# Matrix product with leaky ReLU: the last turn of the first region as two products of quarters, and three measures and sums moved

## The chip, the core and the metric

The kernel runs on one NeuronCore of a Trainium2 chip. The metric is device time in microseconds (us) of one execution. The engines are named as in the profile: PE (TensorE, the matrix multiplier), PEld (its weight loads), DVE (VectorE), ACT (ScalarE), POOL (GpSimd) and SP (SyncE). In this kernel POOL and SP mainly issue DMA transfers; POOL's casting loads bring float32 in as float16.

## The reference

```python
a, b: 4096 x 4096 float32, drawn from a normal distribution; alpha = 0.01
x = np.matmul(a, b)
return np.where(x > 0, x, alpha * x)
```

## The kernel before, in words

**Regions.** The output is cut into 16 regions of 1024 rows by 1024 columns, named (g, j): g is the group of rows, j the pair of column blocks of 512. All of one group is done before the next. The depth of 4096 is cut in two halves of two units of 1024 (KC = 8 slices of 128 each), so that a region's A is 2 x 2 blocks (A11 to A22, each 512 rows by 2048) and its B too (b11 to b22, each 2048 by 512; the first index is the half of the depth, the second the 512 columns).

**Seven products.** All regions but the first are computed by a Strassen-Winograd scheme with seven block products instead of eight. `PRODUCTS` (L684) gives their order: a11 with b11, a12 with b21, s2 with t2, s3 with t3, s1 with t1, a22 with t4, s4 with b22. The s are sums of blocks of A (`sum_a`, L598), the t are sums of blocks of B (`b_sum`, L618); DVE makes both, and t3, t2, t4 and t1 overwrite b12, b11, b21 and t2 in place. A block product is 64 matmuls of 128x512 (L864). From the second group on, many block products are again split into seven products of quarters (`quarter_product`, L781): 16 matmuls of 128x256 each, with further sums of quarters (`sums_of_a`, `sums_of_b`).

**The first region** (0, 0) is computed plainly, as loads come in: `TURNS` lists four turns over the units of the depth, for the upper and the lower 512 rows in turn. Each turn fills all eight PSUM banks; `spill` (L322) then adds a bank to `part[h]`, the float32 tile of the rows of half h, in SBUF. The loop over `steps` (L464) runs over the turns' units; the last turn is its steps 6 and 7, the lower rows with units 2 and 3, that is A22 with b21 and b22: 128 matmuls (L290). During step 5 DVE transposes A22 piece by piece (L143) as its loads land. `leave_first` (L333) puts the result through leaky ReLU; the upper rows are stored by SP at once, the lower ones by POOL at the start of region (0, 1).

**Measures.** The seven-product scheme is used only if the data is even enough: `Measure` (L222) squares a block on ACT (four squares of 128x2048), adds the squares on DVE (L246, L249, L250), folds them (`fold`, L253) and keeps greatest, least and sum in `stats`. A `judge` at the end decides whether a plain product in a second branch is to run instead. `EARLY` and `MEASURED` (L676 and on) say in which region which block is measured. Before, A21 (`first_measure`), b21 and b22 of pair 0 (`last_columns`) are measured in the first region and at the start of (0, 1).

**Order.** Each engine runs its instructions in the order in which the program writes them (`manual_schedule`), and so does each DMA queue; semaphores hold an instruction until what it needs is there. Tiles come from pools with few buffers: `x` (3), `c` (2 for each of two tags), `a16` (3), `b` (2 for each tag). A tile's buffer is written again only when its last reader is done, a DMA that stores it included. So the order of DVE's work ahead of a product, and the stores that it waits for, decide when the product can start.

**Region (0, 1)** (i = 0 in the loop at L819). DVE makes s1, s2, t3 and t2, a measure's sums, s3, the leaky ReLU of the first product, then s4, t4 and t1 (two `b_sum` each). `keep_half` (L833) stores b21 and b22 to DRAM for later groups through SP; t4 overwrites b21. s1 and s2 live in the `x` pool, where the first region's `room` and `part` tiles were.

**Region (1, 0)**, the second of its group: `sums_of_s3` (L760), then `sums_of_a(g, "s1", ...)` (L725, its sums in L736): four sums of quarters of s1 into tiles of the `a16` pool, each stored to DRAM (`kept_qs`); then t3 and t2 for each half of the depth. Region (3, 0) makes the same four sums, but loads its t2 and t3.

**The end.** `seventh_at_the_end` (L1130) computes the last block product by quarters and spreads the adds and leaky ReLUs over it; its last quarter product goes row block by row block (`by_row`).

## Time and profile before

| what | value |
|---|---|
| time, three runs | 1522.14 us median (1522.13 to 1524.24) |
| profiled execution | 1522.71 us, span 1520.9 us |
| mean granted clock | 0.998 |
| first region up to its last turn | 0 to 93.1 us |
| its last turn | 93.1 to 120.7 us |
| region (0, 1) | 120.7 to 221.5 us |
| region (1, 0) | 508.4 to 599.9 us |
| region (3, 0) | 1245.9 to 1335 us |
| last matmul ends | 1513.7 us |

Rows of the timeline give the start in us, the duration in us, the engine, the line of the program, the operation, output <- input with partitions x elements, and the count of merged instructions; in brackets stands how long the engine had been idle before and what ended that. A merged row's duration runs from the first start to the last end. Matmuls are pipelined: a matmul's duration is longer than the distance between two starts, and the distance is what counts. Rows of waits read: who waited <- for whom: us in total, times, longest. Rows that begin with a stretch A:B give its length and the busy time and count of PE, PEld, DVE, ACT and POOL, then the granted PE clock (1.00 is full), the mean busy share of the DMA engines and GB/s. "DMA to landing" gives smallest, median and greatest time from issue to landing of the transfers of one place.

### The profile page before, as it was taken

Reading aid. Unit: us, or ns where it says so; the run is one execution under the profiler, and the core shown is the slowest. Engines: PE = TensorE matmul, PEld = TensorE weight load, DVE = VectorE, ACT = ScalarE, POOL = GpSimd, SP = SyncE. Lnnn points to the kernel's source line nnn. Section 1 sums busy time; section 2 is a strip of 40 time slices with the busy share of each in tenths; the row PEclk is TensorE's granted clock in tenths of the full one; section 3 lists DMA queues with packets and bytes.
Section 4 is the critical chain, followed back from the end, with each engine's and each line's share of the span. In section 5 each row is a group of like instructions: output and inputs, shape, how many; then the busy total and the mean of one; then the engine's idle time right before and its main releaser. Section 6 shows DMA issues by size and latency. Waiting matters only on the chain.

```text
span 1520.9 us, 24417 instructions
## 1 busy us (share of the span) xinstructions
PE 1507.9 (99%) x9883; PEld 965.9 (64%) x9883; DVE 1201.1 (79%) x1250; ACT 524.4 (34%) x905; POOL 252.3 (17%) x418
## 2 busy tenths in 40 slices
PE   9999999999999999999999999999999999999998
PEld 4444444444445667585544688888454488888887
DVE  4589866786697597798779698987887786998797
ACT  2441434647511123225571122323574111242321
POOL 5632110134201102012320101000331000100000
PEclk9999999999999999999999999999999999999999
DMA  9999797899889999999898989979989697987845
GB/s 245 187 217 209 203 277 212 132 215 191 201 346 237 297 290 295 286 293 291 202 259 328 267 319 248 351 241 322 242 215 304 247 279 275 258 293 188 348 146 171
DMA packets 193965, 384.97 MB, mean 253 GB/s; under 512 B 17585, under 2 KB 126385, under 8 KB 178738
## 3 DMA queue, kind: packets, MB, share of 16 engines
q0 software_dynamic: 115584, 108.03, 44.9%
q1 hardware_dynamic: 71058, 245.53, 43.1%
q10 hardware_dynamic: 7200, 29.76, 5.0%
q8 instruction: 79, 1.29, 0.3%
q14 instruction: 44, 0.36, 0.1%
HBM read 359.66 MB, written 129.50 MB: 322 GB/s over the span
## 4 chain that ended last, share of the span: by engine, by line
PE 63%; DVE 1%; DMA 0%; issue 0%; DVEq 0%
PE ps L787 31%; PE ps L864 23%; PE ps L845 9%; DMA s<-kept_s 0%; DVE c L320 0%; DVE b L1354 0%; DVE b L620 0%; DVE c L1144 0%; DVEq L620 0%; DVEq L1144 0%; DVEq L320 0%
## 5 line engine op out<-in xcount | busy, mean ns | idle before, releaser
L864 PE MATMUL ps<-b,a 128*128 128x512 f16 x1984 | 431.6, 379 | 0.0
L864 PEld LDWEIGHTS <-a 128*128 128x128 f16 x1984 | 194.1, 98 | 233.2
L864 PE MATMUL ps<-b,s 128*128 128x512 f16 x1472 | 323.2, 380 | 2.2 <-DVE b L620 2.2
L864 PEld LDWEIGHTS <-s 128*128 128x128 f16 x1472 | 144.4, 98 | 177.0 <-DVE b L620 2.7
L564 POOL DMA_DIRECT2D b<-in_b_dram x120 | 88.9, 746 | 864.2 <-PE ps L864 312.5
L787 PEld LDWEIGHTS <-q 128*128 128x128 f16 x2192 | 214.0, 98 | 26.0 <-issue 0.7
L620 DVE TENSOR_TENSOR b<-b 128x4096 f16<-128x4096 f16 x82 | 185.9, 2286 | 45.0 <-DMA b<-in_b_dram 33.2
L887 ACT COPY c<-ps 128x512 f32<-128x512 f32 x164 | 86.1, 595 | 288.6 <-PE ps L864 187.7
L143 DVE STREAM_TRANSPOSE a<-a 128x512 uint32<-128x512 uint32 (+2 forms) x120 | 126.9, 1105 | 66.7 <-DMA a<-in_a_dram 66.7
L134 POOL DMA_DIRECT2D a<-in_a_dram x252 | 137.4, 552 | 246.6 <-ACT junk L639 82.9
L787 PEld LDWEIGHTS <-a 128*128 128x128 f16 x1440 | 140.9, 98 | 17.4
L320 DVE SCALAR_TENSOR_TENSOR c<-c 128x1024 f32<-128x1024 f32 (+2 forms) x123 | 142.0, 1193 | 10.0 <-ACT c L887 9.7
L639 ACT ACTIVATE junk<-a 128x512 bf16<-128x512 f16 x192 | 121.2, 631 | 70.3 <-DMA a<-in_a_dram 65.1
L787 PE MATMUL ps<-b,q 128*128 128x256 f16 x1088 | 128.1, 273 | 0.0
L237 ACT ACTIVATE sq<-b 128x2048 bf16<-128x2048 f16 x56 | 104.1, 1910 | 63.1 <-DVE sq L246 56.1
L787 PE MATMUL ps<-q,q 128*128 128x256 f16 x1024 | 119.0, 273 | 0.1
L290 PE MATMUL ps<-b,a 128*128 128x512 f16 x512 | 112.2, 379 | 0.5 <-ACT a L387 0.2
L787 PE MATMUL ps<-b,a 128*128 128x256 f16 x912 | 107.4, 273 | 0.0
L787 PEld LDWEIGHTS <-s 128*128 128x128 f16 x960 | 93.9, 98 | 12.3 <-issue 0.9
L290 PEld LDWEIGHTS <-a 128*128 128x128 f16 x512 | 49.7, 98 | 60.8 <-issue 1.4
L845 PE MATMUL ps<-b,a 128*128 128x256 f16 x640 | 70.7, 273 | 0.0
L845 PE MATMUL ps<-b,s 128*128 128x256 f16 x640 | 70.7, 273 | 0.0
(147 smaller groups left out, 1363.7 us busy)
## 6 DMA issues: line engine op xcount, KB each, us to landing
b<-in_b_dram POOLq DMA_DIRECT2D x128, 512.0 KB, 13.6
out_dram<-c SPq DMA_DIRECT2D x118, 512.0 KB, 8.2
a<-in_a_dram POOLq DMA_DIRECT2D x244, 128.0 KB, 5.8
b<-kept_half SPq DMA_DIRECT2D x28, 1024.0 KB, 12.4
b<-kept SPq DMA_DIRECT2D x20, 1024.0 KB, 9.3
q<-kept_qs ACTq DMA_DIRECT2D x40, 512.0 KB, 7.7
s<-kept_s SPq DMA_DIRECT2D x18, 1024.0 KB, 7.2
q<-kept_qs SPq DMA_DIRECT2D x28, 512.0 KB, 6.6
```

Of the source, the lines that this page charges most:

```text
L134: nc.gpsimd.dma_start(a16[32 * q:32 * q + 32], src.rearrange("(g i) w -> i g w", i=32))
L143: nc.vector.transpose(part.rearrange("p c m e -> p c (m e)").bitcast(U32) .rearrange("p c (g i) -> p g c i", i=32), src[:, :, i * n:(i + 1 ...
L237: nc.scalar.activation(to, self.parts[n], SQUARE)
L290: nc.tensor.matmul(ps, a_cols(at[0, h, u], c, mt, (h, u) == (0, 0)), bt[0, u, nt][:, c, :], start=first, stop=last,)
L320: nc.vector.scalar_tensor_tensor(t, t, alpha, t, op0=MULT, op1=MAX if alpha <= 1 else MIN)
L564: nc.gpsimd.dma_start(t[:, c:c + 4, :], b_rows(j, u, c, 4, nt, g > 0))
L620: nc.vector.tensor_tensor(f(to), f(x0), f(x1), op)
L639: nc.scalar.activation(junk, piece[:, q, :], SQUARE, accum_out=to[:, 4 * n + q:4 * n + q + 1])
L787: nc.tensor.matmul(to[m], xq[:, c // 2, rows, c % 2], yq[:, c, :], start=first and c == 0 and m < banks, stop=c == KC - 1, skip_group_chec ...
L845: nc.tensor.matmul(to, a_cols(operand(g, name, k), c, q // 2 * 2 + m), B(half, nt, k)[:, c, q % 2 * HALF:(q % 2 + 1) * HALF], start=False, ...
L864: nc.tensor.matmul(banks[mt], a_cols(t, c, mt, t is first_a), B(half, nt, k)[:, c, :], start=first and (k, c) == todo[0], stop=(k, c) == t ...
L887: nc.scalar.copy(to, bank)
```

## The change

Four things are changed.

1. The last turn of the first region leaves the plain loop. `leave_in_quarters` computes A22 with b21 and A22 with b22 as seven products of quarters each: 14 products of 16 matmuls of 128x256 (224) in place of 128 of 128x512. DVE makes four sums of A22's quarters (`sums`, in tiles of the `c` pool) and three new quarters of b22; those of b21 are made after step 4, in `room`. ACT copies PSUM banks so that a partial result can go on in two places, and `more` adds banks to `part[1]` in SBUF. The leaky ReLU and the stores of `part[0]` come after this turn instead of within it.
2. A21 is measured in (0, 1) instead of in the first region; b21 of pair 0 in (1, 0), ahead of the four sums of s1; b22 of pair 0 in (3, 0), in tiles of the `c` pool, between the third and the fourth of these sums.
3. In (0, 1) the stores of b21 (`keep_half((0,))`) are issued ahead of s3, and s4 is made after t1 instead of before t4.
4. At the end, the last quarter product writes its two row blocks to two banks (one new, `apart`, into which ACT copies what was there) instead of one.

```diff
@@ leave_first
-        if h == 0:
-            nc.sync.dma_start(out[row:row + P, :2 * NT], kept)
-        else:
-            stores.append((out[row:row + P, :2 * NT], kept))
+        nc.sync.dma_start(out[row:row + P, :2 * NT], kept)
@@ the loop over the first region's steps
+    t_of_b21 = {n: room[:, n - 1] for n in range(1, 5)}
...
-    for i in range(1, len(steps)):
+    for i in range(1, len(steps) - last_turn):
...
-            if i == 5 and g > 1:
+            if i == 5 and 1 < g < MT:
                 spill(t, h, leaves, banks)
...
         if i == 4:
             for m in first_columns:
                 m.end()
+            q = quarters_of_first(0)
+            f = lambda n: t_of_b21[n].rearrange("p (c n) -> p c n", n=HALF)
+            nc.vector.tensor_tensor(f(3), q[1, 1], q[0, 1], SUB)
+            nc.vector.tensor_tensor(f(2), f(3), q[0, 0], ADD)
+            nc.vector.tensor_tensor(f(1), q[1, 1], f(2), SUB)
+            nc.vector.tensor_tensor(f(4), q[1, 0], f(2), SUB)
-        if i == 5:
-            first_measure = Measure(0, halves(at[0, 1, 0]) + halves(at[0, 1, 1]), True, room)
-            first_measure.begin()
-            last_columns = [
...
-    last_columns[0].end()
@@ regions in which blocks are measured
     EARLY = {
-        (1, 3): [B11], (1, 1): [B11], (2, 3): [B21], (2, 1): [B12], (3, 1): [B21],
+        (1, 0): [B21], (1, 3): [B11], (1, 1): [B11], (2, 3): [B21], (2, 1): [B12], (3, 1): [B21],
     }
+    IN_C = (3, 0)
@@ sums_of_a
         make(3, (0, 0), (1, 0), SUB)
+        if ahead_of_4:
+            ahead_of_4()
         make(4, (0, 1), 2, SUB)
@@ new
+    def leave_in_quarters():
...
+        for nt in range(2):
+            quarter_product(x[0, 0], b[nt][0, 0], into(chain[nt]), True)
+            nc.scalar.copy(one[nt], chain[nt])
+        for nt in range(2):
+            quarter_product(x[0, 1], b[nt][1, 0], into(one[nt]))
+        tt(fx(1), xf[1, 0], xf[1, 1], ADD)
+        tt(fx(2), fx(1), xf[0, 0], SUB)
+        more(0, 0, 0, one[0])
+        tt(fx(3), xf[0, 0], xf[1, 0], SUB)
+        tt(b[1][0, 1], b[1][1, 1], b[1][0, 1], SUB)
+        tt(fx(4), xf[0, 1], fx(2), SUB)
...
+        new_t(2, turned[1](3), b[1][0, 0], ADD)
+        spill(2, 0, MT - 1, banks)
+        new_t(1, b[1][1, 1], turned[1](2), SUB)
+        for nt in range(2):
+            t = turned[nt]
+            shared, other = new_bank(4 + 2 * nt), new_bank(5 + 2 * nt)
+            if nt == 0:
+                quarter_product(sx(1), t(1), into(shared), True)
+            quarter_product(sx(2), t(2), into(chain[nt]))
+            nc.scalar.copy(other, chain[nt])
+            if nt:
+                quarter_product(sx(1), t(1), into(shared), True)
+            for r in range(2):
+                more(nt, r, 1, shared)
+            quarter_product(sx(3), t(3), into(chain[nt]))
+            if nt:
+                new_t(4, b[1][1, 0], turned[1](2), SUB)
+            more(nt, 1, 1, chain[nt])
+            nc.scalar.copy(one[nt], chain[nt])
+            quarter_product(sx(4), b[nt][1, 1], into(other))
+            more(nt, 0, 1, other)
+            quarter_product(x[1, 1], t(4), into(one[nt]))
+            more(nt, 1, 0, one[nt])
+            if nt == 0:
+                more(1, 0, 0, one[1])
+        for nt in range(2):
+            for r in range(2):
+                leaky(part[1][:, 2 * r:2 * r + 2, nt * NT:(nt + 1) * NT])
+            if nt == 0:
+                for mt in range(MT):
+                    leave_first(0, mt)
...
@@ seventh_at_the_end
+            ends = [of_y(2, 0), part(apart, 0)]
+            nc.scalar.copy(ends[1], of_y(3, 0))
...
-            quarter_product(x[1, 1], t(4), onto(y, 1, 0), by_row=True)
+            quarter_product(x[1, 1], t(4), ends, by_row=True)
@@ the loop over regions
+            c_places = [c_pool.tile([P, 2048], BF16, name="sq", tag=f"c{n % 2}") for n in range(4)]
+            first_measure = Measure(0, halves(at[0, 1, 0]) + halves(at[0, 1, 1]), True, c_places)
+            for n in range(4):
+                first_measure.square(n)
...
+        in_c = (g, j) == IN_C
+        if in_c:
+            m = measure(i, *B22)
+            m.room = [c_pool.tile([P, 2048], BF16, name="sq", tag=f"c{n}") for n in (side, side, 1 - side, 1 - side)]
+            for n in range(4):
+                m.square(n)
+        if second_of_group:
+            sums_of_a(g, "s1", new_a16, m.end if in_c else None)
...
-            last_columns[1].end()
+            first_measure.end()
...
-        if g == 1 and j in OTHERS:
+        if g == 1 and j in OTHERS or (g, j) == (0, LAST):
             keep_half((0,))
...
         if (g, j) == (0, LAST):
-            keep_half()
-        if i == 0:
-            sum_a(g, "s4")
+            keep_half((1,))
...
             for k in ks:
                 b_sum(B(0, 0, k), B(1, 1, k), B(0, 0, k), SUB)
+        if i == 0:
+            sum_a(g, "s4")
```

More of the change, by code (lines that the diff above doesn't have):

```diff
@@ L815, in next_a, with block, more, new_t @@
         return made
+    def leave_in_quarters():
+        x = quarters_of_a(0, "a22")
+        xf = {key: by_chunk(q) for key, q in x.items()}
+        sums = {n: c_pool.tile([P, QUARTER], DT, name="sums", tag=f"c{n % 2}") for n in range(1, 5)}
+        sx = lambda n: a_quarter(sums[n])
+        fx = lambda n: by_chunk(sums[n])
+        b = [quarters_of_first(nt) for nt in range(2)]
+        t3_there = {3: b[1][0, 1]}
+        t_of_b22 = {}
+        turned = [lambda n: b_quarter(t_of_b21[n]), lambda n: t3_there[n] if n in t3_there else b_quarter(t_of_b22[n])]
+        tt = nc.vector.tensor_tensor
+        chain = [new_bank(0), new_bank(2)]
+        one = [new_bank(1), new_bank(3)]
+        def block(nt, r, n):
+            cols = slice(nt * NT + n * HALF, nt * NT + (n + 1) * HALF)
+            return part[1][:, 2 * r:2 * r + 2, cols]
+        def more(nt, r, n, bank):
+            nc.vector.tensor_add(block(nt, r, n), pair(bank), block(nt, r, n))
+        for nt in range(2):
[9 more added lines that the diff above has]
+        tt(fx(4), xf[0, 1], fx(2), SUB)
+        def new_t(n, x0, x1, op):
+            t_of_b22[n] = new_a16()
+            tt(b_quarter(t_of_b22[n]), x0, x1, op)
+        new_t(2, turned[1](3), b[1][0, 0], ADD)
[29 more added lines that the diff above has]
+                    leave_first(0, mt)
+        for mt in range(MT):
+            row = (MT + mt) * P
+            stores.append((out[row:row + P, :2 * NT], part[1][:, mt, :]))
@@ L1128, in first_in_quarters, with seventh_at_the_end @@
                 nc.scalar.copy(z[to], bank)
-        def seventh_at_the_end(y, one, other, tq, sq, one_more):
+        def seventh_at_the_end(y, one, other, tq, sq, one_more, apart):
             pairs, kept = new_c(side)
```

35 lines of the change are left out of this document (13 added, 22 removed).

## The prediction, before the result was known

> **What bounds the kernel now.** I read the table of engines first, then what TensorE (PE) waited for, then the timeline at each place that the diff touches.
>
> ```profile
> PE 1507.9 (99%) x9883; PEld 965.9 (64%) x9883; DVE 1201.1 (79%) x1250; ACT 524.4 (34%) x905; POOL 252.3 (17%) x418
> PE ps L864 <- DVE b L620: 2.2, 1, 2.2
> PE ps L787 <- DVE b L1354: 0.7, 1, 0.7
> 175.60:179.02 3.42, 1.20 (x6) 0.37 (x5) 3.42 (x3) 0.00 (x0) 1.48 (x2) 1.00 1.08 349
> 179.02:182.43 3.41, 3.41 (x9) 1.22 (x8) 3.31 (x3) 0.74 (x1) 0.00 (x0) 0.50 1.14 194
> ```
>
> PE sets the time: 99% busy, and two waits of note in the whole span, 2.2 us in region (0,1) and 0.7 us in (1,0). The two stretches (duration; PE, PEld, DVE, ACT, POOL busy; clock; DMA share; GB/s) show what the first wait drags behind it: PE worked 1.20 of 3.42 us, and in the next 3.41 us the granted clock was 0.50. So time comes only from fewer matmuls, from those waits, or from the tail; and any new wait of VectorE (DVE) ahead of a product is paid in full, perhaps with a stretch at half clock.
>
> **The change, part by part.** The sum is made against the profiled execution, 1522.71 us (span 1520.9); the runs' median, 1522.14, lies 0.6 lower.
>
> *1. The last turn.*
>
> ```profile
> 99.80 21.10 PE L290 MATMUL ps<-b,a 128*128 128x512 f16 x97
> 120.73 27.79 PE L864 MATMUL ps<-b,a 128*128 128x512 f16 x128
> 1485.51 1.91 PE L787 MATMUL ps<-b,q 128*128 128x256 f16 x16
> 1487.25 1.91 PE L787 MATMUL ps<-q,a 128*128 128x256 f16 x16
> 1487.45 0.58 ACT L938 COPY c<-ps 128x512 f32<-128x512 f32 x1 [0.62 <-PE ps L787]
> 72.98 0.71 POOL L194 DMA_DIRECT2D b<-in_b_dram  x1 [0.34 <-DMA b<-in_b_dram]
> DMA to landing us min/median/max: 10.0/10.0/10.0
> 86.99 2.11 DVE L143 STREAM_TRANSPOSE a<-a 128x512 uint32<-128x512 uint32 x2 [5.46 <-DMA a<-in_a_dram]
> 89.60 2.10 DVE L143 STREAM_TRANSPOSE a<-a 128x512 uint32<-128x512 uint32 x2 [0.49 <-DMA a<-in_a_dram]
> 97.15 2.10 DVE L143 STREAM_TRANSPOSE a<-a 128x512 uint32<-128x512 uint32 x2
> 515.64 1.22 DVE L736 TENSOR_TENSOR q<-s 128x2048 f16<-128x2048 f16 x1
> ```
>
> Starts are 20.93/97 = 0.216 us apart for 512 columns, 1.74 us for a product of 16 at 256. The old turn is 128 x 0.216 = 27.6 us, from 93.1 to 120.7; the new one 14 x 1.74 = 24.4. Saved: 3.2.
>
> Two waits come back. The first four products end at 93.1 + 7.0 = 100.1; the fifth needs the first sum of A22, and DVE has turned the last piece of A22 at 99.25. Ahead of that DVE gets four quarters of b21 that need a load issued at 72.98 and landing 10.0 later, at 83.0; 4 x 1.22 end at 87.9, 0.9 past the 86.99 at which it took up A22; the next piece had waited 0.49 for its own load, so 0.4 is left. So 99.25 + 0.4 + 1.22 = 100.9: PE waits 0.7 to 0.8. Then the product with sum 3 writes the bank that ScalarE (ACT) has just begun to copy, with nothing between: ACT starts 0.2 after a product's last start and takes 0.58 (row at 1487.45 against 1487.25), so 0.8. The rest is in time: the first sum of b22 is DVE's sixth after 100.9 (107.4), and PE comes to it at 110.4. If ACT's copy were hidden the waits would be 0.7, and if the loads came another us late, 2.5. Net: 3.2 - 1.5 = **-1.7**, the turn ending at 119.0.
>
> *2. Region (0,1).*
>
> ```profile
> 100.33 4.63 DVE L320 SCALAR_TENSOR_TENSOR part<-part 128x1024 f32<-128x1024 f32 x4
> DMA to landing us min/median/max: 6.9/7.7/8.7
> 104.86 1.23 DVE L246 TENSOR_TENSOR room<-room 128x2048 bf16<-128x2048 bf16 x1
> 111.77 1.28 DVE L331 TENSOR_TENSOR part<-ps,part 128x512 f32<-128x512 f32 x2
> 134.15 6.62 DVE L590 TENSOR_TENSOR s<-s,a 128x4096 f16<-128x4096 f16 x2
> 143.16 6.88 DVE L620 TENSOR_TENSOR b<-b,b 128x4096 f16<-128x4096 f16 x3 [0.19 <-issue]
> 156.37 6.62 DVE L590 TENSOR_TENSOR a<-a,a 128x4096 f16<-128x4096 f16 x2
> 165.18 4.48 DVE L590 TENSOR_TENSOR s<-a,s 128x4096 f16<-128x4096 f16 x2
> 170.99 2.29 DVE L620 TENSOR_TENSOR b<-b,b 128x4096 f16<-128x4096 f16 x1 [1.32 <-DMA kept_half<-b]
> 173.82 6.70 DVE L620 TENSOR_TENSOR b<-b,b 128x4096 f16<-128x4096 f16 x3 [0.54 <-DMA kept_half<-b]
> 178.37 15.68 PE L864 MATMUL ps<-b,s 128*128 128x512 f16 x64 [2.22 <-DVE b L620]
> 536.04 13.98 PE L864 MATMUL ps<-b,s 128*128 128x512 f16 x64
> ```
>
> The 2.2 us wait is for t1: DVE made s4 first (4.48) and then twice stood behind the stores of b21 (1.32 + 0.54). Both go: s4 comes after t1, and those stores are issued before s3. t1 stands 6.3 us nearer to s3. Gone with the wait are the 15.68 - 13.98 = 1.7 us at half clock (the row at 536.04 is a product of the same form at full clock): **-3.9**.
>
> But DVE enters the region fuller. After the turn it still has an add (to 119.9), then eight passes of leaky at 1.16. The sixth, at 126.9, releases the last of four stores of part[0], whose buffer s2 overwrites; the store rows give 6.9 to 8.7 to land, the last ones longest, so s2 starts at 135.6 instead of 134.15. From there as in the rows: the first half of t2 is done 11.3 later, 146.9, and PE asks at 119.0 + 27.6 = 146.6 (0.3); s3 follows 15.9 + 6.9 (the measure of A21, 104.86 to 111.77) after s2's start, its first half 3.3 later, 161.7, and PE asks at 160.7 (1.0). Bounds: 0 at 6.9 to land, and some 3 if it takes two us longer than any row. I take **+1.3**, by the 8.7. t1 is then ready at about 174, PE asks at 175.5: spare 1.5.
>
> The measures that left the first region cost nothing there before, and their squares on ACT are off the path; s4, at 179 instead of 170, is asked for only at 203. SP's early stores stand behind part[0]'s stores and ahead of region outputs that wait for s3 anyway.
>
> *3. b21 measured in (1,0).*
>
> ```profile
> 494.91 1.48 POOL L564 DMA_DIRECT2D b<-in_b_dram  x2 [0.26 <-PE ps L787]
> DMA to landing us min/median/max: 19.6/21.2/22.9
> 508.42 27.79 PE L864 MATMUL ps<-b,a 128*128 128x512 f16 x128
> 525.25 1.23 DVE L736 TENSOR_TENSOR q<-s,q 128x2048 f16<-128x2048 f16 x1 [5.99 <-DMA kept_qs<-q]
> kept_qs<-q SPq DMA_DIRECT2D x1, 512.0 KB, 6.5
> 530.84 2.29 DVE L620 TENSOR_TENSOR b<-b 128x4096 f16<-128x4096 f16 x1 [4.37 <-DMA b<-in_b_dram]
> 607.25 1.91 ACT L237 ACTIVATE sq<-b 128x2048 bf16<-128x2048 f16 x1 [0.66 <-DVE sq L246]
> 609.20 1.23 DVE L250 TENSOR_TENSOR sq<-sq 128x2048 bf16<-128x2048 bf16 x1 [0.65 <-ACT sq L237]
> 612.84 0.34 DVE L271 TENSOR_TENSOR stats<-stats,r 128x16 f32<-128x16 f32 x3
> ```
>
> Times here are those of before; all of it moves with PE, whose products release the loads. DVE idles 10.4 us between 519 and 531, but not in one piece: the fourth sum of s1 (525.25) waits for the store of the first (515.64 + 1.22), because its buffer is reused: 8.4 us. The measure stands ahead of the first sum. Its fourth square needs the half of b21 that lands last, 495.65 + 22.9 = 518.5; 1.9 on ACT makes 520.5; the third add to the end takes 609.20 to 613.18, 4.0: the first sum starts at 524.5 instead of 515.64, its store at 525.7. In this stretch such stores took 8.4 (behind two region outputs) and 6.5 (the fourth sum's, at 526.5); the second is the nearest in time and queue, so 532.2. Fourth sum to 533.4, t3 to 535.7, t2 to 538.0; PE asks at 536.04: a wait of **+2.0**. Bounds: none if it lands in 4, 3.9 at 8.4. The old 0.7 us wait at 552.5 goes (**-0.7**), as PE comes later and DVE hardly does. Queued behind the late sum are the second half of s2 (a load) and SP's three loads of sums of s1; both have spare for 2 us. By the row of (0,1), where 2.2 us of waiting was followed by 3.41 us at 0.50, I add **+1.7**.
>
> On this a rule of the Trainium skill speaks for the other side: "TensorE: Matmul & The Clock Gate", Part 1, has the clock fall only after an idle window of about 3.4 us; by it this wait stays at full clock and the sum is 1.7 lower. The trace differs: a window with PE busy 1.20 of 3.42 us sufficed.
>
> *4. b22 in (3,0), and the end.*
>
> ```profile
> 1269.23 1.23 DVE L736 TENSOR_TENSOR q<-s,q 128x2048 f16<-128x2048 f16 x1 [7.09 <-DMA kept_qs<-q]
> 1513.83 0.42 DVE L1144 TENSOR_TENSOR c<-ps,c 128x256 f32<-128x256 f32 x1 [0.65 <-PE ps L787]
> 1515.08 0.42 DVE L320 SCALAR_TENSOR_TENSOR c<-c 128x256 f32<-128x256 f32 x1
> ```
>
> In (3,0) the measure sits in the 7.09 us that DVE waits before the fourth sum; by my estimate it ends some 2 us late, and what follows has that spare. **Nothing**; uncovered it would be a wait like that of (1,0). At the end the two last rows of blocks sat in one bank, so both adds waited for the last matmul; in two banks the first add and leaky (0.42 each) run beside the last eight matmuls. Between nothing and 0.85 I take **-0.6**, since DVE comes from an earlier leaky.
>
> Sum: -1.7 - 3.9 + 1.3 + 2.0 - 0.7 + 1.7 - 0.6 = -1.9, so 1520.8 on the profile and **1520.2** against the median.
>
> **The rivals.** *A, the wait in (1,0) without half clock:* for it, 2.0 us can straddle two windows, and the 0.7 us wait left the clock at full; against it, the row of (0,1). 1520.2 - 1.7 = 1518.5. *B, no wait in (1,0):* the store lands in 4 us, as the queue is emptier than it was for the store of 516.9; then the old 0.7 stays. 1520.2 - 2.0 - 1.7 + 0.7 = 1517.2. *C, the change doesn't do what it says in (0,1):* DVE, late from part[0]'s stores, misses t1 by as much as before; spare is only 1.5. Up to 3.9 given back: 1524.1. *D, slower:* the loads of b21 in (1,0) are held by DMA and not by PE, so they land when they did before although PE comes 4.3 us sooner (1.7 + 3.9 - 1.3). The wait is 6.3 and takes two windows of half clock: 1520.2 + 4.3 + 1.7 = 1526.2. It loses to before from a wait of about 4 us. Against it: POOL issued each of these loads upon a release by PE.
>
> **How the numbers follow.** About 0.2% (3.0 us) is what a measurement tells from no change: 1519.1 to 1525.2. Forecast (1519.1 to 1522) 0.36, A 0.22, B 0.14, C 0.14, D 0.09, something that I don't see 0.05. Faster: A, B and a share of the rest, 0.40; slower: D and a little, 0.10; same 0.50. The range 1516.5 to 1524.5 holds all but part of B and D; the forecast's own is 1519 to 1522.
>
> **What would show it.** In the profile after: product 0 of (0,1) starting at 119 (step 1); no wait of PE on L613 ahead of the product with s1, at most 1 us at those of t2 and s3 (step 2); in (1,0) the fourth sum waiting on its store, and PE some 2 us on t2, followed by a stretch at 0.50 (step 3); the last leaky 0.6 nearer to the last matmul (step 4). A wait over 4 us in (1,0), or the clock at 0.50 in the first region, makes the forecast wrong; so does a (1,0) without a wait.

## The result, and the profile after

| kernel | median of runs | spread | ratio to before (95% interval) |
|---|---|---|---|
| before | 1522.06 us (13 runs) | 1519.79 to 1525.88 | |
| after | 1526.05 us (13 runs) | 1522.42 to 1529.09 | 1.0026 (1.0019 to 1.0034) |

The change makes the kernel slower by 0.26%, 4.0 us. The profiled execution of after took 1526.61 us (span 1524.8, granted clock 0.998), that of before 1522.71 (span 1520.9): 3.9 apart, so the two traces show what the medians show. The runs of one kernel spread over 6 us, so medians of a dozen runs don't settle a difference of one us. A trace can show such a difference at one place, but it is of one execution, and a wait in it need not be in the next.

First the page's table of engines for after, then what PE waited for in it (us in total, times, longest).

```profile
PE 1506.4 (99%) x9979; PEld 975.6 (64%) x9979; DVE 1217.0 (80%) x1266; ACT 528.3 (35%) x912; POOL 252.4 (17%) x418
PE ps L932 <- DVE b L613: 4.5, 3, 1.8
PE ps L781 <- ACT ps L867: 3.6, 2, 3.4
PE ps L932 <- DVE a L583: 1.8, 1, 1.8
PE ps L781 <- DVE sums L838: 0.8, 1, 0.8
PE ps L781 <- ACT ps L858: 0.7, 1, 0.7
```

PE's busy time fell by 1.5 us, but its waits grew from two of note (2.2 and 0.7) to eight, 11.4 us in all. PE's timeline says where the largest lie.

```profile
93.34 7.15 PE L781 MATMUL ps<-b,a 128*128 128x256 f16 x64
101.30 3.67 PE L781 MATMUL ps<-room,sums 128*128 128x256 f16 x32 [0.81 <-DVE sums L838]
105.62 1.91 PE L781 MATMUL ps<-room,sums 128*128 128x256 f16 x16 [0.66 <-ACT ps L858]
107.37 1.91 PE L781 MATMUL ps<-b,sums 128*128 128x256 f16 x16
112.65 3.39 PE L781 MATMUL ps<-room,a 128*128 128x256 f16 x16 [3.37 <-ACT ps L867]
...
124.99 27.79 PE L932 MATMUL ps<-b,a 128*128 128x512 f16 x128
154.60 13.97 PE L932 MATMUL ps<-b,s 128*128 128x512 f16 x64 [1.82 <-DVE b L613]
170.42 13.99 PE L932 MATMUL ps<-b,a 128*128 128x512 f16 x64 [1.85 <-DVE a L583]
...
541.36 13.97 PE L932 MATMUL ps<-b,s 128*128 128x512 f16 x64 [0.97 <-DVE b L613]
633.56 13.97 PE L932 MATMUL ps<-b,s 128*128 128x512 f16 x64 [1.70 <-DVE b L613]
...
1517.84 1.91 PE L781 MATMUL ps<-q,s 128*128 128x256 f16 x16
```

The last turn runs from 93.34 to 124.99, 31.65 us in place of 27.6. It holds the two waits that were foreseen (0.81 and 0.66) and one of 3.37 that was not; the product behind that wait takes 3.39 in place of 1.91, at half clock (0.50 from 112.31 to 115.73).

In (0,1) the product with t2 waits 1.82 us and that with s3 1.85, where before had 2.22 at t1 and 1.7 us at half clock. In (1,0) there is a wait of 0.97 at t2 at full clock, and the old one of 0.74 is gone; in (1,3) there is a new one of 1.70.

The account of the span, after minus before: a later start of the turn, +0.2; the turn, +4.0; t2 and s3 in (0,1), +3.7; t1 there, -3.9; (1,0), +0.2; (1,3), +1.7; the end, -0.7 from the last product's start to the last leaky and -1.4 from there to the end of the last store. Together +3.8 of 3.9. Where the 1.4 at the very end comes from was not found.

**Why 3.37.** Of ACT's and DVE's timelines in the turn, the rows around that wait:

```profile
112.03 0.57 ACT L867 COPY ps<-ps 128x512 f32<-128x512 f32 x1 [6.45 <-DVE part L831]
```

```profile
100.02 1.23 DVE L838 TENSOR_TENSOR sums<-a,a 128x2048 f16<-128x2048 f16 x1
...
109.89 2.70 DVE L831 TENSOR_TENSOR part<-ps,part 128x512 f32<-128x512 f32 x4
116.15 1.29 DVE L831 TENSOR_TENSOR part<-ps,part 128x512 f32<-128x512 f32 x2 [3.56 <-PE ps L781]
...
143.24 6.63 DVE L583 TENSOR_TENSOR s<-s,a 128x4096 f16<-128x4096 f16 x2 [3.81 <-DMA out_dram<-part]
```

The copy that PE waits for (L867, one bank to another) reads the bank that the product with sum 3 has filled by 107.4. It starts at 112.03, 4.6 us later, and what released it is no matmul but DVE's add (L831). DVE reads the same bank for `part[1]`, and the program writes that add ahead of the copy. The add is the third of the row at 109.89; DVE has worked without a gap since 100.02, on sums that later products need and on adds of earlier banks. After it DVE itself idles 3.56 us for PE: the two engines wait for each other in turn, and DVE's total work is not the limit. The last row is s2 in (0,1): it waits 3.81 us for the last store of part[0], which makes t2 and s3 late. Two rows on lines of the program give the sizes. For the stores of part[0] (L337) it is smallest, median and greatest time from issue to landing; for s3 (L583) smallest, median and greatest duration in ns of its two instructions, and the first and last start:

```profile
DMA to landing us min/median/max: 7.8/8.5/9.5
L583 DVE TENSOR_TENSOR a<-a,a x2: 2283/3350/4416, 165.9 to 170.3; 128x4096 f16<-128x4096 f16 x2
```

The first half of s3 takes 4.4 us and the second 2.3, so PE can start on s3 4.4 us after DVE does.

### The profile page after: what moved, and what is told of

Same layout as the page of the kernel before. It is cut to its first block, busy times and chain, and to the rows that moved or that the text cites. A ratio compares the mean times of both kernels' runs of the same rounds, so it can differ in the third digit from the quotient of the medians.

```text
span 1524.8 us, 24638 instructions
## 1 busy us (share of the span) xinstructions
PE 1506.4 (99%) x9979; PEld 975.6 (64%) x9979; DVE 1217.0 (80%) x1266; ACT 528.3 (35%) x912; POOL 252.4 (17%) x418
## 4 chain that ended last, share of the span: by engine, by line
PE 64%; DVE 1%; issue 0%
PE ps L781 31%; PE ps L932 24%; PE ps L913 9%; DVE b L613 0%; DVE c L1214 0%; DVE c L320 0%; DVE s L799 0%
## 5 line engine op out<-in xcount | busy, mean ns | idle before, releaser
L932 PE MATMUL ps<-b,a 128*128 128x512 f16 x1984 | 431.7, 379 | 1.8 <-DVE a L583 1.8
L932 PEld LDWEIGHTS <-a 128*128 128x128 f16 x1984 | 194.0, 98 | 235.2 <-DVE a L583 2.3
L955 ACT COPY c<-ps 128x512 f32<-128x512 f32 x164 | 86.3, 595 | 287.4 <-PE ps L932 153.7
L781 PEld LDWEIGHTS <-a 128*128 128x128 f16 x1536 | 151.0, 98 | 23.3 <-issue 3.9
L237 ACT ACTIVATE sq<-b 128x2048 bf16<-128x2048 f16 x60 | 111.5, 1911 | 63.4 <-DVE sq L246 51.9
L781 PE MATMUL ps<-q,q 128*128 128x256 f16 x1024 | 119.0, 273 | 0.0
L781 PE MATMUL ps<-b,a 128*128 128x256 f16 x976 | 114.5, 273 | 0.0
L781 PEld LDWEIGHTS <-s 128*128 128x128 f16 x960 | 93.9, 98 | 11.4
L290 PE MATMUL ps<-b,a 128*128 128x512 f16 x384 | 84.7, 379 | 0.4
L960 DVE TENSOR_TENSOR c<-ps,c 128x512 f32<-128x512 f32 x76 | 47.0, 679 | 30.3 <-PE ps L932 30.3
L913 PE MATMUL ps<-b,a 128*128 128x256 f16 x640 | 70.7, 273 | 0.0
```

The lines of the kernel that those rows point to most:

```text
L237: nc.scalar.activation(to, self.parts[n], SQUARE)
L290: nc.tensor.matmul(ps, a_cols(at[0, h, u], c, mt, (h, u) == (0, 0)), bt[0, u, nt][:, c, :], start=first, stop=last,)
L781: nc.tensor.matmul(to[m], xq[:, c // 2, rows, c % 2], yq[:, c, :], start=first and c == 0 and m < banks, stop=c == KC - 1, skip_group_chec ...
L913: nc.tensor.matmul(to, a_cols(operand(g, name, k), c, q // 2 * 2 + m), B(half, nt, k)[:, c, q % 2 * HALF:(q % 2 + 1) * HALF], start=False, ...
L932: nc.tensor.matmul(banks[mt], a_cols(t, c, mt, t is first_a), B(half, nt, k)[:, c, :], start=first and (k, c) == todo[0], stop=(k, c) == t ...
L955: nc.scalar.copy(to, bank)
```

## The experiments

**1. ACT's copy ahead of DVE's add; two parts of the change alone; no measure of b21.**

```diff
 e1_copy_ahead: after, leave_in_quarters
-            more(nt, 1, 1, chain[nt])
             nc.scalar.copy(one[nt], chain[nt])
+            more(nt, 1, 1, chain[nt])
 e2_only_01_and_end: before, with part 3 and part 4 of the change
+        if g == 1 and j in OTHERS or (g, j) == (0, LAST):
             keep_half((0,))
...
-        if i == 0:
-            sum_a(g, "s4")
         for k in [] if in_fourth else ks[1:] if turning and g else ks:
             b_sum(B(1, 0, k), B(1, 0, k), B(0, 0, k), SUB)
...
                 b_sum(B(0, 0, k), B(1, 1, k), B(0, 0, k), SUB)
+        if i == 0:
+            sum_a(g, "s4")
 e3_no_b21_measure: after
-        (1, 0): [B21], (1, 3): [B11], (1, 1): [B11], (2, 3): [B21], (2, 1): [B12], (3, 1): [B21],
+        (1, 3): [B11], (1, 1): [B11], (2, 3): [B21], (2, 1): [B12], (3, 1): [B21],
```

> The kernel after, with one change in the last turn: ScalarE's copy of the chain bank (L867 of the kernel after) is written ahead of VectorE's add of the same bank, in place of behind it. Theory (the copy waited for VectorE only because it was written behind VectorE's add of the same bank): the copy starts when the product with sum 3 ends, near 107.5 us; the wait of 3.37 us at the product with x11 and the half clock behind it go; region (0,1) starts at 119.5 to 120 in place of 124.99, and as nothing behind it changes, the time is 5 less than the kernel after: near 1521. Rival 1 (VectorE's work in the turn is the true bound): the wait moves on to a later product of the turn, (0,1) still starts at 123 or later and the time is 1524 to 1526. Rival 2 (the start of (0,1) gains, but VectorE and the stores of part[0] don't move with it): the waits of 1.82 and 1.85 us at t2 and s3 grow to 4 each, one of them followed by half clock, and the time is 1524 again.

Measured: median 1523.84 us (12 runs), ratio to before 1.0014 (1.0006 to 1.0023), profiled span 1519.3. PE's timeline of this kernel:

```profile
104.19 1.91 PE L781 MATMUL ps<-room,sums 128*128 128x256 f16 x16 [0.66 <-ACT ps L858]
105.93 1.91 PE L781 MATMUL ps<-b,sums 128*128 128x256 f16 x16
107.67 1.91 PE L781 MATMUL ps<-room,a 128*128 128x256 f16 x16
...
118.16 20.88 PE L932 MATMUL ps<-b,a 128*128 128x512 f16 x96
...
154.03 7.07 PE L932 MATMUL ps<-b,s 128*128 128x512 f16 x32 [0.77 <-DVE b L613]
165.26 15.68 PE L932 MATMUL ps<-b,a 128*128 128x512 f16 x64 [4.17 <-DVE a L583]
```

The product with `x[1, 1]`, the one that had waited 3.37, follows without a gap, and (0,1) starts at 118.16 in place of 124.99. So the written order of two readers of one bank was the cause of the wait of 3.37, and the first rival falls. The second is half right: in (0,1) the wait at s3 grows to 4.17, with half clock behind it (15.68 in place of 13.98). That gives back 0.77 + 4.17 + 1.7 - 3.7 = 3.0 of the 6.4 that the turn became shorter. The time is a miss for the theory, which had 1521: by the ratios this kernel is only about 1.8 us below after, with intervals that overlap a little, and it is still slower than before.

> The kernel before, with two parts of the change alone: the order of region (0,1) (s4 behind t1, the stores of the first half of b21 and b22 issued before s3) and the separate bank at the end. The last turn and the measures are those of the kernel before. Theory: the wait of 2.22 us at t1 and the half clock behind it (together 3.9) go, the last leaky stands 0.5 nearer to the last matmul, nothing else moves: 1522.1 - 3.9 - 0.5 = 1517.7. Rival 1 (the wait at t1 came from something other than s4 and the two stores, as VectorE's work in this region is the bound): a wait of 1 to 2 us stays at t1 or at a later product, and the time is 1520 to 1521.5. Rival 2 (the half clock has nothing to do with the wait): only the wait goes, 1519.4.

Measured: median 1520.51 (11 runs), ratio 0.9985 (0.9976 to 0.9994), profiled span 1515.6. The wait at t1 and the stretch at half clock are gone, but a new one stands ahead of s3:

```profile
163.56 13.99 PE L864 MATMUL ps<-b,a 128*128 128x512 f16 x64 [1.34 <-DVE a L590]
```

So part 3 works, and brings something of its own that makes DVE late at s3. The time, 1.7 us below before, and a wait that moved to a later product are what the first rival said; its reason, that DVE's own work is the bound, is not what DVE's timeline shows:

```profile
143.05 2.29 DVE L620 TENSOR_TENSOR b<-b,b 128x4096 f16<-128x4096 f16 x1 [0.19 <-issue]
148.08 4.68 DVE L620 TENSOR_TENSOR b<-b,b 128x4096 f16<-128x4096 f16 x2 [2.74 <-DMA b<-in_b_dram]
```

In before the three sums from 143.16 on ran without a gap; now the second waits 2.74 us for a load of b.

> The kernel after without the measure of pair 0's b21 in region (1,0); that measure is left out altogether. Theory: the wait of 0.97 us at t2 in (1,0) goes and the old wait of 0.7 us at t3's or s1's product comes back: 0.2 to 0.3 less than the kernel after, not to be told from it by the time, but to be seen in PE's waits. Rival (the wait in (1,0) stems from the loads of b21, not from the measure): the wait of 0.97 us stays where it is.

Measured: median 1524.51 (11 runs), ratio 1.0011 (1.0003 to 1.002). The wait at t2 in (1,0) is gone and one of 0.47 stands at the place of the old one. So the rival falls in this trace. The ratio is 0.0015 below that of after, but the intervals meet; experiment 4 asks again with another pair of kernels. This kernel has the first region of after, and its trace is a second record of the fault in the turn:

```profile
111.38 1.91 PE L781 MATMUL ps<-room,a 128*128 128x256 f16 x16 [3.11 <-ACT ps L867]
```

The wait is there again, but full clock behind it; the turn takes 28.92 us (93.32 to 122.24), where after's took 31.65. So of the 4.0 that the turn costs in after's trace, a part is not there in every run. The profiled executions of these three kernels are each the fastest of their runs, so the other runs hold some lost time that these traces don't show.

**2. Where the waits of (0,1) come from.** Three edits of e1_copy_ahead, and one of e2_only_01_and_end:

```diff
 e4_measure_behind_s3
-        if i == 0:
-            first_measure.end()
...
         if first_of_group:
             sum_a(g, "s3")
+            if i == 0:
+                first_measure.end()
 e5_late_stores_of_b21; the same in e7_01_end_late_stores
-        if g == 1 and j in OTHERS or (g, j) == (0, LAST):
+        if g == 1 and j in OTHERS:
             keep_half((0,))
...
         u1_pairs, _ = keep(z, side)
+        if (g, j) == (0, LAST):
+            keep_half((0,), nc.scalar)
 e6_part0_out_sooner
                 more(1, 0, 0, one[1])
+                leave_first(0, 0)
...
             more(nt, 1, 1, chain[nt])
+            if nt:
+                leave_first(0, 1)
             quarter_product(sx(4), b[nt][1, 1], into(other))
             more(nt, 0, 1, other)
+            if nt:
+                leave_first(0, 2)
+                leave_first(0, 3)
...
-            if nt == 0:
-                for mt in range(MT):
-                    leave_first(0, mt)
```

> The kernel of the copy put ahead (e1_copy_ahead), in which VectorE's adds of the measure of A21 (about 7 us, ahead of s3 in region (0,1)) stand behind s3. Theory (PE's wait of 4.17 us at the product with s3, and the half clock behind it, come from VectorE's queue, where that measure is ahead of s3): s3's first half is ready 7 us sooner, near 157, PE asks for it near 161: the wait and the stretch at half clock go, 5.9 less than that kernel's profile (span 1519.3, so near 1513.4), with the wait of about 0.8 at t2 left. Rival (the loads and stores decide, not the order on VectorE): s3's wait stays above 2 us.

Measured (one run): 1526.35, span 1524.5, against a span of 1513.4 expected. PE's timeline:

```profile
166.35 1.07 PE L932 MATMUL ps<-b,a 128*128 128x512 f16 x2 [5.27 <-ACT c L955]
167.63 15.97 PE L932 MATMUL ps<-b,a 128*128 128x512 f16 x62 [0.20 <-ACT c L955]
...
542.51 13.97 PE L932 MATMUL ps<-b,s 128*128 128x512 f16 x64 [2.94 <-DVE b L613]
```

s3 was ready sooner (DVE took it up at 153.88 in place of 160.79), and PE now waited 5.27 us for ACT's copies (L955) of the previous product into the `c` tiles. Those tiles hold the measure's squares until DVE has folded them. Neither the theory nor the rival, by which loads and stores decide, is what happened: the measure of A21 holds two things, DVE's queue and the `c` tiles, and cannot simply be put later.

> The kernel of the copy put ahead (e1_copy_ahead), in which the two early stores of b21 in region (0,1) are issued from ScalarE's queue behind its copies of the second product (near 160) in place of from SyncE's near 126. Theory (the DMA engines are at work without a break until near 150, and the 2 MB of early stores push back the load for which VectorE waited 3.16 us at 149.30): that wait goes, the wait of 0.77 at t2 goes with it and that at s3 shrinks from 4.17 to about 1, without half clock: 5 less than that kernel's span of 1519.3, near 1514.5. Rival (that load is late because of the order of the loads themselves or of the stores of part[0]): VectorE waits 2 us or more for it as before, and PE at s3 3 to 4 us.

Measured (one run): 1519.73, span 1517.8. DVE's three sums run without a gap again from 146.38, so the load no longer comes late. PE waits 0.61 at t2 and 1.86 at s3, without half clock. That is less than the theory had (no wait at t2, about 1 at s3). The span is 1.5 below that of e1_copy_ahead and not 5; part of the gain is hidden, as in this run the turn began 0.9 later and took 1.3 longer, and t2 in (1,0) waited 0.9 longer (1.43). What is left in (0,1) is the wait of s2 for the last store of part[0]:

```profile
137.36 6.63 DVE L583 TENSOR_TENSOR s<-s,a 128x4096 f16<-128x4096 f16 x2 [2.66 <-DMA out_dram<-part]
```

> The kernel of the copy put ahead (e1_copy_ahead), in which the four leaky passes and stores of part[0] are spread over the second half of the last turn in place of standing behind it. Theory (s2 waited 2.29 us, in the kernel after 3.81 us, for the last store of part[0], and by that DVE was late for t2 and s3): the wait of s2 goes; as VectorE next waits for the load of b, PE's waits at t2 and s3 stay within 1 us of 0.77 and 4.17. Rival 1 (the passes in the turn delay a sum that PE needs there): a new wait of 1 us or more in the last turn. Rival 2 (the stores are all that makes VectorE late): the waits at t2 and s3 fall by 2 us or more together.

Measured (one run): 1526.44, span 1524.6. DVE's timeline first, then PE's:

```profile
130.27 6.62 DVE L583 TENSOR_TENSOR s<-s,a 128x4096 f16<-128x4096 f16 x2
137.16 2.29 DVE L613 TENSOR_TENSOR b<-b,b 128x4096 f16<-128x4096 f16 x1 [0.27 <-DMA b<-in_b_dram]
139.64 2.29 DVE L613 TENSOR_TENSOR b<-b,b 128x4096 f16<-128x4096 f16 x1 [0.19 <-PE ps L935]
149.94 4.68 DVE L613 TENSOR_TENSOR b<-b,b 128x4096 f16<-128x4096 f16 x2 [8.01 <-DMA b<-in_b_dram]
```

```profile
165.91 15.51 PE L935 MATMUL ps<-b,a 128*128 128x512 f16 x64 [4.17 <-DVE a L583]
...
526.87 15.66 PE L935 MATMUL ps<-b,a 128*128 128x512 f16 x64 [3.30 <-ACT ps L1333]
```

As the theory has it: s2 waits no longer, and the whole gain is lost to the load of b, which lands no sooner than in e1_copy_ahead (149.94 against 149.30). The two late things stand one behind the other. Mending the store of part[0] alone shows nothing at PE; mending the load alone (e5_late_stores_of_b21) took 2.3 us off the wait at s3, and the half clock with it. The second row of PE was not expected: in (1,0) b21 landed late in this run, ACT's squares for its measure stood ahead of the bank copies (L1333), and PE waited 3.30 us. That is the fourth of the rivals that were put up, in a form in which ACT and not DVE is in the way.

> The kernel before with the order of (0,1) and the bank at the end alone (e2_only_01_and_end), and the two early stores of b21 issued from ScalarE's queue behind its copies of the second product. Theory (as for e5_late_stores_of_b21): VectorE's wait of 2.74 us on the load of b goes, and PE's wait of 1.34 at s3 with it; the span falls from 1515.6 to about 1514.3, with the wait at t1 no more than 0.5. Rival (late stores bring the wait at t1 back, as t1's sums overwrite what is stored): a wait of 1.5 us or more at t1.

Measured (one run): 1516.05, span 1514.2; no wait of PE in (0,1) at all, neither at s3 nor at t1. This kernel differs from e2_only_01_and_end only in when, and from which queue, 2 MB of stores are issued. The windows show what these stores met; before first, then e2_only_01_and_end, then this kernel. Region (0,1) starts within 0.2 us of 120.7 in all three:

```profile
142.00:148.00 6.00, 6.00 (x30) 2.71 (x28) 5.72 (x4) 0.00 (x0) 0.00 (x0) 1.00 0.93 355
148.00:154.00 6.00, 6.00 (x30) 2.70 (x29) 5.90 (x5) 0.00 (x0) 0.00 (x0) 1.00 0.01 3
```

```profile
142.00:148.00 6.00, 6.00 (x29) 2.73 (x28) 3.15 (x2) 0.00 (x0) 0.00 (x0) 1.00 1.11 343
148.00:154.00 6.00, 6.00 (x29) 2.74 (x28) 5.80 (x4) 0.00 (x0) 0.00 (x0) 1.00 0.63 257
```

```profile
142.00:148.00 6.00, 6.00 (x30) 2.70 (x29) 5.72 (x4) 0.00 (x0) 0.00 (x0) 1.00 0.74 299
148.00:154.00 6.00, 6.00 (x29) 2.71 (x28) 5.90 (x5) 0.00 (x0) 0.00 (x0) 1.00 0.00 0
```

The last two numbers of a row are the mean busy share of the DMA engines (as this view counts it, 1.24 is the most that occurs here) and GB/s. In before and in this kernel DMA has work up to about 148 and then none; with the early stores it works on for some 4 us more. Among what came later is the load that DVE waits for: its sum starts 27.5 us after the start of (0,1) in e2_only_01_and_end, and 30.3 to 31.4 in e1_copy_ahead, e4_measure_behind_s3 and e6_part0_out_sooner, all with the early stores. With the late stores it starts 24.9 to 26.4 after it in the traces in which DVE had to wait for the load at all (e9_all_mended, e9_again and e10_mended_no_b21_measure below).

**3. The best of it, timed.**

> The same kernel as e7_01_end_late_stores (the kernel before with the order of (0,1), the bank at the end and the late stores of b21; no quarters in the last turn, measures where they were), now timed. Theory (the order of (0,1) and the end are worth 3.9 + 0.5, and only the early stores took 1.3 of it back): the median is 4 to 5 below the kernel before of the same chip, ratio 0.9970 to 0.9975, and 2 to 3 below that of e2_only_01_and_end against its own runs of before. Rival (the one look was lucky, the early stores cost nothing in most runs): ratio 0.998 to 0.999, as e2_only_01_and_end.

Measured: median 1517.15 (8 runs), ratio 0.9972 (0.9961 to 0.9982): parts 3 and 4 with the late stores gain 4.5 us, as the theory has it (0.9970 to 0.9975); its profile too has no wait of PE in (0,1). What the early stores alone cost is less sure: e2_only_01_and_end was at 0.9985, some 2 us above, but the two intervals overlap, and this one's upper end touches the rival's 0.998.

> The kernel after with its three faults in the first region mended together: ScalarE's copy ahead of VectorE's add, part[0] out in the course of the last turn, the early stores of b21 on ScalarE's queue behind the copies of the second product. Theory (s2's wait for part[0]'s stores and t2's wait for the load of b, both pushed by transfers in a stretch in which DMA has no idle time, are what is left in (0,1)): no wait above 0.5 in (0,1), the turn 25 to 26 long, and the wait in (1,0) of 0.5 to 1.5 left; the median 3.5 to 5 below before, ratio 0.9968 to 0.9977. Rival 1 (two loads or stores late at once, as DMA is full: part[0]'s stores, now sooner, hold up the loads again): a wait of VectorE of 2 us or more for b, PE's wait at s3 above 1 us, ratio 0.998 to 1. Rival 2 (b21 in (1,0) lands late in most runs, and ScalarE's squares hold the copies of the banks, 3.3 us as in e6_part0_out_sooner): nothing is gained over before, ratio 0.999 to 1.001.

Measured: median 1516.72 (9 runs), ratio 0.9966 (0.9955 to 0.9977), span 1515.2. PE's timeline:

```profile
107.06 1.91 PE L781 MATMUL ps<-b,sums 128*128 128x256 f16 x16
108.80 1.91 PE L781 MATMUL ps<-room,a 128*128 128x256 f16 x16
...
119.28 27.79 PE L935 MATMUL ps<-b,a 128*128 128x512 f16 x128
146.91 13.98 PE L935 MATMUL ps<-b,s 128*128 128x512 f16 x64
161.62 13.99 PE L935 MATMUL ps<-b,a 128*128 128x512 f16 x64 [0.73 <-DVE a L583]
```

The turn ends at 119.28 after 26.3 us (25 to 26 expected), the wait at t2 is gone, that at s3 is 0.73, a little over the 0.5 expected, and (1,0) has 1.41. Half of the first rival came true: DVE still waits for the load of b, 3.37 us here (2.85 and 1.88 in the two profiles of experiment 4), but it comes to it so early that PE hardly notices. This kernel, the whole change with three edits, is 9 us under after and faster than both kernels of the comparison; by the median it is 0.4 under e8_01_end_late_stores_timed, which the runs can't tell from nothing. So the turn in quarters and the moved measures, once mended, are together worth next to nothing over the order of (0,1) and the end alone.

**4. b21's measure, and the end, by themselves.** The kernel of e9_all_mended with the diff of e3_no_b21_measure, beside itself; and before with part 4 of the change alone.

```diff
 e10_mended_no_b21_measure: e9_all_mended
-        (1, 0): [B21], (1, 3): [B11], (1, 1): [B11], (2, 3): [B21], (2, 1): [B12], (3, 1): [B21],
+        (1, 3): [B11], (1, 1): [B11], (2, 3): [B21], (2, 1): [B12], (3, 1): [B21],
 e11_only_the_end: before
+            ends = [of_y(2, 0), part(apart, 0)]
+            nc.scalar.copy(ends[1], of_y(3, 0))
...
-            quarter_product(x[1, 1], t(4), onto(y, 1, 0), by_row=True)
+            quarter_product(x[1, 1], t(4), ends, by_row=True)
```

> The kernel of e9_all_mended once more, beside the next one on the same chip. Both theories: its ratio is again 0.9955 to 0.9977.

> The kernel of e9_all_mended without the measure of pair 0's b21 in region (1,0), which is left out altogether. Theory (the measure costs PE about 1.4 at t2 in (1,0) in a typical run, and saves a wait of 0.7 later): the wait of 1.41 goes, one of 0.5 to 0.7 comes at 552, and the median is 0.5 to 1.5 below that of e9_again. Rival 1 (in many runs b21 lands late and ScalarE's squares hold the bank copies, 3.3 us and half clock as in e6_part0_out_sooner): the median is 2 to 4 lower. Rival 2 (it costs nothing in the median): the same within 0.5.

Measured: e9_again 1517.01 (6 runs), ratio 0.9971 (0.9959 to 0.9984); e10_mended_no_b21_measure 1516.78 (5 runs), ratio 0.9963 (0.995 to 0.9977). The medians are 0.2 apart, which is what the second rival says, but five and six runs that spread over 6 us don't rule out the 0.5 to 1.5 of the theory. In the profiles the wait at t2 in (1,0) was 0.97, 0.51, 2.94, 1.43, 1.41 and 0.41 us with the measure (and the 3.30 at another product). In six profiles without it there was none, but e11_only_the_end, the next kernel, which has no measure there either, has this row; DVE's row says why:

```profile
543.61 7.07 PE L864 MATMUL ps<-b,s 128*128 128x512 f16 x32 [2.06 <-DVE b L620]
```

```profile
538.94 4.62 DVE L620 TENSOR_TENSOR b<-b 128x4096 f16<-128x4096 f16 x2 [5.97 <-DMA b<-in_b_dram]
```

PE waited 2.06 us for the second half of t2, since a load of b landed late. So a wait at t2 in (1,0) can come from the loads alone, and what the measure costs changes from run to run, with no price that these runs can tell.

> The kernel before with the separate bank at the end alone. Theory (the first of the two last adds runs beside the last eight matmuls): from the start of the last product to the end of the last leaky 2.95 us in place of 3.69, and nothing else moves: 0.7 less than before, ratio 0.9993 to 0.9998. Rival (the tail of the stores is shorter too: in the profile of before 5.4 us lay between the last leaky and the end of the span, in those of kernels with the separate bank 4.0 to 4.4): 2 less, ratio near 0.9987.

Measured: median 1521.22 (11 runs) beside 1521.26, ratio 0.9998 (0.9989 to 1.0007). From the start of the last product (1513.20) to the end of the last leaky (1516.15) it is 2.95 us, against 3.69 in before, as expected; from there to the end of the span it is 5.15 here, so nothing in this profile speaks for the rival, by which the separate bank shortens the tail too (it is 4.0 to 4.4 in the other kernels that have it, which all have part 3 as well). The profile of this kernel, which has (0,1) as before, shows one thing more:

```profile
178.50 13.99 PE L864 MATMUL ps<-b,s 128*128 128x512 f16 x64 [2.23 <-DVE b L620]
```

It is the wait at t1 of before, as long as there (2.23, there 2.22), in the same place, but the product behind it takes 13.99 us and not 15.68: the clock stays at 1.00. The last section says why.

## Why the prediction was wrong, point by point

**Step 1, the last turn: wrong, and the main loss.** The step that failed is "The rest is in time". It put each sum against the product that reads it, and found the two waits of 0.7 to 0.8 (measured 0.81 and 0.66). It did not put the second copy of ACT against what is ahead of it: that copy waits for a DVE add of the same bank, and DVE had a row of other work ahead of the add. The Trainium skill states such an order: "PSUM — Partial Sum Buffer", in its section on bank collisions, says of the compiler's scheduler that it makes two instructions of different engines on one bank dependent, reads alike, ACT and DVE among them. The row at 112.03 and e1_copy_ahead agree. This cost 3.37 and the half clock behind it; the turn ended at 124.99 and not at 119.0. The prediction had named the clock at 0.50 in the first region as a sign of being wrong, and there it was, though e3_no_b21_measure shows that the half clock was bad luck and the wait was not. e1_copy_ahead, with the two lines exchanged, takes 25.3 us for the turn, against the 25.9 of the prediction (24.4 + 1.5), so the rest of the term was right.

**Step 2, region (0,1): t1 as forecast, t2 and s3 mis-sized.** The wait at t1 went by the mechanism that was given, and e8_01_end_late_stores_timed measures 4.5 for it and the end together against 4.5 expected (3.9 and 0.6). That the two agree so well is partly luck, as 1.7 of the 3.9 is half clock that not every run of before has. For t2 and s3 the mechanism was right (s2 waits for the last store of part[0]), but the term was 1.3 and measured 1.82 + 1.85 = 3.7, past its bound of 3 too. Two of its pieces were too small. The last store was issued at 132.8 and took 9.5 us to land, and s2 started at 143.24, 0.9 later: 10.4 from the store's issue to s2, where the prediction had 8.7 from the end of the leaky pass to s2. And the first half of s3 was put at 3.3 us, half of a merged row of 6.62, when it takes 4.4. In the trace of before, too, the first half of s3 (156.37) takes 4.42. The early stores of b21 are not what made part[0]'s store land late: it took at most 7.9 us in e1_copy_ahead with them and 8.0 in e5_late_stores_of_b21 without. Why it took 9.5 in after stays open. The sentence that the early stores cost nothing as they stand "behind part[0]'s stores" looked at the queue and not at the loads beside them: e2_only_01_and_end (1.34 at s3) and e7_01_end_late_stores (nothing) show their price there.

**Step 3, b21 in (1,0): the mechanism right, the size too large.** The fourth sum of s1 waited for its store as described; PE waited 0.97 at t2 and not 2.0, the old 0.74 went, and the half clock did not come. The first sum began at 528.20, where the forecast's 524.5 with PE's 4.2 us would be 528.7, and its store and the wait for it took 6.1 in place of 6.5. By the medians the step costs nothing that these runs can tell. The rival of late loads of b21 did occur once, in e6_part0_out_sooner. By the rule of the Trainium skill that was weighed there ("TensorE: Matmul & The Clock Gate", Part 1: the clock falls after an idle window of about 3.4 us) the half clock should have been left out, and it did stay away.

**Step 4: (3,0) free, as forecast; the end right in size, and too small to be seen** (0.74 in the trace against 0.6; ratio 0.9998). The wait of 1.70 in (1,3) had no step; it stands behind a load of b that landed late (DVE waited 11.49 for it, 9.45 in before), and in the other profiles it is between nothing and 0.5. Why it came late is not known.

Against the profile the forecast was 1520.8 and 1526.6 came: +5.8 from the turn, +2.4 from t2 and s3, -2.8 from (1,0), +1.7 from (1,3), -1.5 from the end. Rival D gave nearly the measured time, 1526.2, but its mechanism, late loads of b21 in (1,0), is not what made after slow: there the wait was 0.97. That the time agrees is luck.

## What to carry to other kernels

Where a result in PSUM is read by two engines, write the reader that the matrix engine waits for first: the other one's whole queue may stand ahead of it. Here it stood 4.6 us ahead of the copy. Before moving a store, look at the busy share of DMA in the stretch that it is moved to, and at what lands there: here 2 MB of stores made a load late enough for DVE to wait 2.74 us. A merged row of two instructions is not twice one of them: here the halves took 4.4 and 2.3. And when two late things stand one behind the other, mending one of them can show nothing: here it took both before PE's waits in (0,1) were down to 0.7 and less.

## What the runs showed of the hardware

**The clock behind a wait depends on where the wait falls in a grid of 3.413 us.** Behind a wait of 2.22 us the next 3.41 us had the clock at 0.50 (before), behind one of 2.23 at the same product it stayed at 1.00 (e11_only_the_end). Over all these kernels, waits of 2.06, 2.23, 2.94 and 3.11 us were followed by full clock, and those of 2.22, 3.30, 3.37, 4.17 (twice) and 5.27 by a stretch at half.

The traces hold the times at which the granted clock changed, and these settle it. In before they are 4.94, 179.02, 182.43 and 1517.04 us: 51, 1 and 391 steps of 3.413 us apart. In every one of the 14 traces all changes lie a whole number of such steps apart, but the first one lies anywhere from 3.86 (e11_only_the_end) to 7.08 us (e7_01_end_late_stores) after the start. So the clock changes on a grid that is not tied to the kernel. Before's wait at t1 falls into one window of its grid, 175.60 to 179.02, with PE busy for 1.20 us. In e11_only_the_end the boundary falls into the wait, and each window gets a part of it:

```profile
174.53:177.94 3.41, 1.74 (x9) 0.59 (x6) 3.41 (x2) 0.00 (x0) 0.74 (x1) 1.00 1.04 349
177.94:181.35 3.41, 2.85 (x14) 1.32 (x15) 3.41 (x3) 0.00 (x0) 0.74 (x1) 1.00 1.09 229
```

The same for the other long waits, with the window of the run's own grid in which PE was busy least:

| run | wait of PE | window | PE busy in it | clock in the next |
|---|---|---|---|---|
| e4_measure_behind_s3 | 5.27 | 162.27 to 165.68 | 0.00 | 0.50 |
| e6_part0_out_sooner | 4.17 | 162.19 to 165.61 | 0.00 | 0.50 |
| after | 3.37 | 108.90 to 112.31 | 0.38 | 0.50 |
| e1_copy_ahead | 4.17 | 162.36 to 165.78 | 0.52 | 0.50 |
| e6_part0_out_sooner | 3.30 | 524.01 to 527.42 | 0.55 | 0.50 |
| before | 2.22 | 175.60 to 179.02 | 1.20 | 0.50 |
| e3_no_b21_measure | 3.11 | 106.56 to 109.97 | 1.72 | 1.00 |
| e11_only_the_end | 2.23 | 174.53 to 177.94 | 1.74 | 1.00 |
| e11_only_the_end | 2.06 | 539.75 to 543.16 | 1.80 | 1.00 |
| e4_measure_behind_s3 | 2.94 | 537.74 to 541.15 | 1.83 | 1.00 |

Cut along its grid from the first change to the last, each trace has some 440 windows. In all of them the clock fell behind a window at full clock with PE busy for 1.20 us or less, and never behind one with 1.55 or more; none lies between. From this an estimate: a single wait under some 1.8 us (3.41 - 1.55) won't bring half clock, one over 4.4 (twice 3.41 - 1.20) always will, and between them it depends on the run. The Trainium skill ("TensorE: Matmul & The Clock Gate", Part 1) says that the window is free-running, 3413 ns long, and that an idle one brings half clock: the traces agree with the first two, but the wait of 2.22 shows that a window in which PE was busy for a third can be enough. For this case it means that of the 3.9 us that t1 cost in before, 1.7 were not there in every run.
